# A head's values are split inside the head that uses them, and the attention weights' tiles are taken later

## The chip, the cores and the metric

The kernel runs on one core of one Trainium2 chip. The metric is the device time of one execution in microseconds (us), as the median of several runs. Short names in what follows: PE is TensorE (matmuls), PEld its weight loads, DVE is VectorE, ACT is ScalarE, POOL is GpSimd, SP is SyncE, whose queue issues most of the loads.

## The reference

One step of a two-layer trunk over a prompt of 512 frames and eight samples of 16 frames each. Layer 0 is a gated linear recurrence. Its output is projected once to keys and values, and layer 1 is stick-breaking attention over 16 heads of 128 columns. The change touches only layer 1's attention. Cut to that:

```python
def sb_block(q, q_pos, k, v):
    z = einsum('bqhd,bshd->bhqs', q, k) * HEAD_DIM ** -0.5
    mask = arange(S)[None, :] < q_pos[:, None]
    log_keep  = where(mask, log_sigmoid(-z), 0.0)
    log_after = cumsum(log_keep, axis=3, reverse=True) - log_keep
    attn = where(mask, exp(log_sigmoid(z) + log_after), 0.0)
    return einsum('bhqs,bshd->bqhd', attn, v)

def stick_breaking_mixer(hn, k_all, v_all, w_in, w_out):
    q, zg = split(hn @ w_in, 2)
    o = stick_breaking(heads(q), k_all, v_all)
    return (o * silu(zg)) @ w_out
```

The prompt attends to itself (512 keys). Each sample attends to 512 cached keys and its own 16.

## The kernel before

Every float32 product that has to be exact is made of three matmuls. An operand x is split into a high part xh, which ACT writes as a rounded copy, and a low part xl = x - xh, which DVE writes by a subtraction; `mm3` then adds sh·mh, sh·ml and sl·mh. A split is therefore always one ACT copy and, behind it, one DVE subtraction.

`heads` runs the 16 heads one after the other. The work of a head is cut into steps with one-letter names, and two strings, `ORDER` for heads 0 to 14 and `LAST` for head 15, write out in which order they are traced. The letters:

- P (`prompt_scores`): the scores of the prompt in three matmul groups z3, z2, z1, and for each the chain `sticks`: on ACT Abs, Exp, Ln; on DVE an add, a scan and a subtraction; on ACT the closing Exp (L1664, kept in `self.weighed`); on POOL a mask. The results are the tiles e3, e2, e1.
- q: the next piece of the generator `query(h + 1)`, the product of the next head's query and gate. Its matmuls carry the name psh. A piece gets its weights from splits (L1376 to L1380) that the function `fill` issues ahead. Partial sums leave PSUM by copies on ACT (L1542, `keep`) or sums on DVE (L1547, `evac`), and the PSUM bank is written again by the next partial product.
- c and C (`sample_close`), X (`new_scores`), S0 and S1 (`sample_scores`, again with the chain of `sticks`), V (`prompt_turn`: e3, e2, e1 are transposed on PE and split into the tiles ath and atl, L1748 and L1749), T (`sample_turn`), O (`prompt_out`: the product of ath, atl with the values vh, vl), M (`sample_out`).
- L, K: the next head's keys are loaded and split. U: the next head's values are loaded (`values_load`, L1682, tile vr). W: the next head's values are split (`values_split`, L1326 and L1328, tiles vh and vl). N: the first cached keys of the next head are loaded.

The tile vr of the loaded values has the tag ath and that tag has one buffer. So the values' load can only start when O has read the attention weights of the same head out of it, and the attention weights of the next head can only be written when the values have been split out of it.

A framework keeps the order: each engine works its queue first in, first out; the queues are filled by priority, which follows the order of tracing (raised within `high_priority`), with its own estimate of when things are ready. `issue_after(x)` puts the instructions of a block behind x on x's engine. `self.scaled` is the last copy of the next query on ACT (L1460), `self.weighed` the latest closing Exp.

In the kernel before, W stands near the end of a head, between N and the last q, and its copy is to come behind `self.scaled`. On ACT's queue it has landed behind the first Abs of the next head's P.

Of the kernel before, what the change touches and what calls it, by code (L numbers as in the profile page):

```python
# [13 lines left out]
F32R = mybir.dt.float32r  # L14
# [6 lines left out]
P = 128  # L21
# [4 lines left out]
T = 640  # L26
# [20 lines left out]
X12, X22, X11, S1, S2, S3, S4 = range(7)  # L47
# [4 lines left out]
class Trunk:  # L52
# [12 lines left out]
    def ring(self, tag, bufs, name):  # L65
        return self.pp.tile([P, 512], F32, tag=tag, name=name, bufs=bufs)
# [701 lines left out]
    S0 = 3 + TP  # L768
# [932 lines left out]
    def attention(self, h, ap, qkv, zs):  # L1701

        nc, I, O = self.nc, self.I, self.O
        V, A, mm, tr = nc.vector, nc.scalar, nc.tensor.matmul, nc.tensor.transpose
# [2 lines left out]
        one = self.bank  # L1707
        zt = lambda n: self.ring("quad", 4, n)
        pd = "p (t d) -> p t d"
        qh, ql, qs, kh, kl, knT, vh, vl = qkv  # L1710

        def score(out, i, first):
            q = slice(P * i, P * i + P)
# [1 line left out]
            mm(out, qh[:, q], kh[:, :n], start=first, stop=False, **kw)  # L1715
            mm(out, qh[:, q], kl[:, :n], start=False, stop=False, **kw)
            mm(out, ql[:, q], kh[:, :n], start=False, stop=True, **kw)

        ath = ap.tile([P, 2 * T], F32R, tag="ath", name="ath", bufs=1)
        atl = ap.tile([P, 2 * T], F32R, tag="atl", name="atl", bufs=1)  # L1720

        def turned(x, i):

            if i == 0:
                return x[:, 0:P]
            return x[:, P:].rearrange("p (m s) -> p m s", s=FIRST)[:, : min(i + 1, 3), P * (i - 1) : P * i]

        def block(x, i):

            return x[:, 896:1024] if i == 3 else x[:, TP * i : FIRST * i + TP]  # L1730

        def spread(e, *rows, ring=one):

            ps = ring("pa")
            n = sum(i + 1 for i in rows)
            for j in range(n):
                tr(ps[:, P * j : P * j + P], e[:, P * j : P * j + P], self.ident)
            parts, c = [], 0
            for i in rows:
                m = min(i + 1, 3)  # L1740
                src = ps[:, c : c + P * m]
                parts.append((src.rearrange(pd, d=P) if i else src, turned(ath, i), turned(atl, i)))
                if i == 3:
                    parts.append((ps[:, 384:], block(ath, 3), block(atl, 3)))
                c += P * (i + 1)
            with self.tc.high_priority(200):
                for sv, hv, lv in parts:
                    self.turned = A.activation(hv, sv, AF.Copy).ins  # L1748
                    V.tensor_tensor(lv, sv, hv.bitcast(F32), ALU.subtract)  # L1749
# [15 lines left out]
        def new_values():  # L1765
            t = ap.tile([TS, NB, P], F32, tag="vn", name="vn", bufs=1)
            dma(t, O["v"][TP:, P * h : P * h + P].rearrange("(b t) d -> t b d", t=TS))
            return t
# [84 lines left out]
            A.activation(zn, ps[:, : 2 * TS], AF.Copy)  # L1853

        def prompt_turn():
            spread(st["e3"], 3)
            spread(st["e2"], 2, 0)
            spread(st["e1"], 1, ring=zt)

        def prompt_out():  # L1860
            po = zt("po")
            for i in range(3, -1, -1):
                th, tl = block(ath, i), block(atl, i)
                self.mm3(po[:, P * i :], vh[:, i, :], vl[:, i, :], th, tl, i == 3, i == 0, **kw)
            V.tensor_tensor(o[:, :TP], po, zs[:, :TP], ALU.mult)
# [3 lines left out]
        if h == NHEAD - 1:  # L1869
            o = self.outs.tile([P, 2, 3 * HALF], F32R, tag="ks1", name="o", bufs=1)[:, 0, :T].bitcast(F32)  # L1870
        st = {"vn": new_values()}
        steps = {"P": prompt_scores, "V": prompt_turn, "X": new_scores, "O": prompt_out, "T": sample_turn, "M": sample_out, "C": sample_close}
        for g in range(2):
            steps[f"S{g}"] = lambda g=g: sample_scores(g)
# [2 lines left out]

    STAY = (NHEAD - 2,)
    WHOLE = tuple(range(14))
    LAST = "P c X S0 q q q S1 V q q q q Z T O M q C q"  # L1880
    ORDER = "P q q c X S0 q q q S1 V q q L q T O U K M N W q"

    def heads(self, count=NHEAD):
        with self.pool("att") as ap:
            self.attention_consts(ap)
            self.qraw, self.qready = [None] * 4, {"wh": [], "wl": []}
            for i in (0, 1, 3, 2):
                self.query_load(0, i)
            self.qplan = {"wh": self.product_plan(), "wl": self.plain_plan()}
            out = self.attention_begin()  # L1890
            keys = self.keys_load(0, ap)
            self.ck = self.cached_keys(0, 0, ap)
            self.first_query(ap)
            values = self.values_load(0, ap)
            k, v = self.keys_split(ap, keys), self.values_split(ap, values)
            before = {}
            for h in range(count):
                qh, ql, qs, zs = self.q
                steps = self.attention(h, ap, (qh, ql, qs, *k, *v), zs)
                more = h + 1 < count  # L1900
                qn = self.query(h + 1, ap) if more else out
                if not more:
                    self.behind = self.turned
                for step in (self.ORDER if more else self.LAST).split():
                    if step == "q":
                        next(qn, 0)
                    elif step == "Z":
                        for j in range(2):
                            self.silu(ap, zs, j)
                    elif step in steps:  # L1910
                        steps[step]()
                    elif step == "c":
                        before.get(step.upper(), lambda: None)()
                    elif more and step == "L":
                        keys = self.keys_load(h + 1, ap)
                    elif more and step == "U":
                        values = self.values_load(h + 1, ap)
                    elif more and step == "N":
                        self.ck = self.cached_keys(h + 1, 0, ap)
                    elif more and step == "K":  # L1920
                        with self.tc.issue_after(self.weighed):
                            k = self.keys_split(ap, keys)
                    elif more:
                        with self.tc.issue_after(self.scaled):
                            v = self.values_split(ap, values)
                before = steps
        return out

# [111 lines left out]
def lay_out(r):  # L2040

    heads = lambda v, b: v.reshape(b, -1, NHEAD, P)
    y, k, v = r["y"], r["kT"].T, r["v"]
    state = r["state"].transpose(2, 1, 0).reshape(36, DR)
    out = [y[:TP].reshape(1, TP, D), y[TP:].reshape(NB, TS, D), heads(k[:TP], 1), heads(v[:TP], 1), heads(k[TP:], NB),
           heads(v[TP:], NB), state[0:1].reshape(1, 1, DR), state[1:9].reshape(1, NB, DR),
           state[9:12].reshape(1, 1, 3, DR), state[12:].reshape(1, NB, 3, DR)]
    return tuple(np.ascontiguousarray(v) for v in out)
# [14 lines left out]
```

## Time and profile before

| | |
|---|---|
| median of 3 runs | 2855.23 us (2852.07 to 2855.8) |
| profiled execution | 2849.34 us, its span 2847.6 us |
| granted TensorE clock, mean | 0.997 |
| PE, DVE, ACT busy over the span | 97%, 71%, 58% |
| attention heads 1 to 14 | from 2048.5 to 2600.5 us of the span, 37.6 to 41.5 us each |
| in these 552.0 us | PE busy 536.1 us, DVE 416.4 us, ACT 359.7 us |

The page's busy shares are means over stages with different limits; the heads are the stage that the change touches. In a view by windows each row is a stretch of time with the busy time of each engine in it. In a timeline each row is an instruction: start, duration, engine, line, operation, tiles, and in brackets how long its engine sat idle before it and what ended the wait. A row of the waits names who waited for whom, the sum in us, the number of times and the longest. ACT and DVE instructions are shown with overlapping ends: the next one starts before the shown end of the one before.

### The profile page before, as it was taken

Reading aid. Unit: us, or ns where it says so; the run is one execution under the profiler, and the core shown is the slowest. Engines: PE = TensorE matmul, PEld = TensorE weight load, DVE = VectorE, ACT = ScalarE, POOL = GpSimd, SP = SyncE. Lnnn points to the kernel's source line nnn. Section 1 sums busy time; section 2 is a strip of 40 time slices with the busy share of each in tenths; the row PEclk is TensorE's granted clock in tenths of the full one; section 3 lists DMA queues with packets and bytes.
Section 4 is the critical chain, followed back from the end, with each engine's and each line's share of the span. In section 5 each row is a group of like instructions: output and inputs, shape, how many; then the busy total and the mean of one; then the engine's idle time right before and its main releaser. Section 6 shows DMA issues by size and latency. Waiting matters only on the chain.

```text
span 2847.6 us, 47819 instructions
## 1 busy us (share of the span) xinstructions
PE 2775.1 (97%) x18340; PEld 2457.2 (86%) x18340; DVE 2031.0 (71%) x3312; ACT 1656.7 (58%) x2846; POOL 414.1 (15%) x702
## 2 busy tenths in 40 slices
PE   6999999999999999999999999999999999999998
PEld 4799999999999987777787899967898888987887
DVE  7677776777677765766866866667877777778335
ACT  5467555666566555765756555553666666667223
POOL 0012222222122211111120000122100000001000
PEclk9999999999999999999999999999999999999999
DMA  8966676667666666585686333585465665658536
GB/s 314 343 145 149 166 164 159 150 161 164 161 154 157 157 209 215 192 261 171 222 297 218 102 108 115 174 271 200 137 197 174 203 182 171 194 176 282 165 110 229
DMA packets 244166, 535.31 MB, mean 188 GB/s; under 512 B 22536, under 2 KB 106632, under 8 KB 242784
## 3 DMA queue, kind: packets, MB, share of 16 engines
q1 hardware_dynamic: 198320, 372.99, 41.5%
q0 software_dynamic: 45616, 159.26, 22.9%
q8 instruction: 144, 2.36, 0.3%
q14 instruction: 86, 0.70, 0.1%
HBM read 495.39 MB, written 36.78 MB: 187 GB/s over the span
## 4 chain that ended last, share of the span: by engine, by line
PE 78%; DVE 5%; DMA 4%; ACT 3%; issue 2%; POOL 0%; SPq 0%; DVEq 0%; POOLq 0%; ACTq 0%
PE acc L112 6%; PE acc L114 6%; PE acc L113 6%; PE pa L112 4%; PE pa L114 4%; PE pa L113 4%; PE psh L112 4%; PE psh L114 3%; PE psh L113 3%; PE pc L114 3%; PE pc L112 3%; PE pc L113 3%; DMA vr<-out_v_dram 3%; PE acck L112 3%; PE acck L113 2%; PE acck L114 2%
## 5 line engine op out<-in xcount | busy, mean ns | idle before, releaser
L112 PE MATMUL acc<-wh,yh 128*128 128x512 f32 x940 | 370.2, 394 | 0.0
L113 PE MATMUL acc<-wl,yh 128*128 128x512 f32 x940 | 366.5, 390 | 1.5 <-DVE wl L98 1.5
L114 PE MATMUL acc<-wh,yl 128*128 128x512 f32 x940 | 365.5, 390 | 1.3 <-DVE yl L969 1.3
L98 DVE TENSOR_TENSOR wl<-wr,wh 128x1024 fp32r<-128x1024 f32 x151 | 186.0, 1237 | 208.5 <-ACT wh L97 208.3
L97 ACT ACTIVATE wh<-wr 128x1024 fp32r<-128x1024 f32 x151 | 159.7, 1058 | 259.5 <-PE acc L114 213.1
L112 PEld LDWEIGHTS acc<-wh,yh 128*128 128x128 f32 x940 | 176.4, 188 | 53.6 <-issue 16.7
L113 PEld LDWEIGHTS acc<-wl,yh 128*128 128x128 f32 x940 | 176.5, 188 | 38.9 <-DVE wl L98 3.5
L114 PEld LDWEIGHTS acc<-wh,yl 128*128 128x128 f32 x940 | 176.4, 188 | 38.7 <-DVE yl L969 1.7
L202 DVE TENSOR_TENSOR wa<-wa 128x1024 bf16<-128x1024 f32 (+1 forms) x160 | 191.3, 1247 | 8.9 <-ACT wa L201 8.5
L114 PE MATMUL pa<-xs,wl 128*128 128x320 f32 x630 | 194.8, 309 | 0.5 <-DVE wl L98 0.5
L113 PE MATMUL pa<-xs,wh 128*128 128x320 f32 x630 | 194.7, 309 | 0.0
L112 PE MATMUL pa<-xs,wh 128*128 128x320 f32 x630 | 194.7, 309 | 0.0
L97 ACT ACTIVATE wh<-sum 128x896 fp32r<-128x896 f32 x102 | 96.8, 949 | 143.7 <-PE pa L113 46.8
L201 ACT ACTIVATE wa<-wa 128x1024 bf16<-128x1024 f32 x160 | 159.3, 1046 | 23.0 <-DVE wa L202 11.4
L112 PE MATMUL psh<-nh,wl 128*128 128x320 f32 x480 | 149.8, 312 | 1.9 <-DVE z L1547 1.9
L553 POOL DMA_DIRECT2D sum<-w_in_a_dram x90 | 79.1, 882 | 497.8 <-DVE wl L98 211.2
L114 PE MATMUL psh<-nh,wl 128*128 128x320 f32 x480 | 148.3, 309 | 0.0
L113 PE MATMUL psh<-nl,wl 128*128 128x320 f32 x480 | 148.3, 309 | 0.0
L97 ACT ACTIVATE wh<-rv 128x256 fp32r<-128x256 f32 (+1 forms) x108 | 51.8, 479 | 146.1 <-PE pa L113 95.8
L114 PE MATMUL pc<-xs,wl 128*128 128x320 f32 x420 | 129.8, 309 | 0.7 <-DVE wl L98 0.7
L112 PE MATMUL pc<-xs,wh 128*128 128x320 f32 x420 | 130.0, 310 | 0.0
L113 PE MATMUL pc<-xs,wh 128*128 128x320 f32 x420 | 129.8, 309 | 0.0
(490 smaller groups left out, 8538.3 us busy)
## 6 DMA issues: line engine op xcount, KB each, us to landing
wa<-w_ada_dram POOLq DMA_DIRECT2D x120, 512.0 KB, 5.0
wr<-w_out_a_dram SPq DMA_DIRECT2D x96, 512.0 KB, 4.3
sum<-w_in_a_dram POOLq DMA_DIRECT2D x90, 448.0 KB, 5.6
wa<-w_ada_dram SPq DMA_DIRECT2D x72, 512.0 KB, 6.8
wr<-w_in_b_dram SPq DMA_DIRECT2D x64, 512.0 KB, 4.4
ck<-cache_k_dram SPq DMA_DIRECT2D x64, 512.0 KB, 5.8
wr<-w_out_b_dram SPq DMA_DIRECT2D x55, 512.0 KB, 3.9
raw<-w_in_a_dram SPq DMA_DIRECT2D x60, 448.0 KB, 4.4
```

The source lines that it names most:

```text
L97: self.split_at = nc.scalar.activation(hi[:, :n], raw, AF.Copy).ins
L98: nc.vector.tensor_tensor(lo[:, :n], raw, hi[:, :n].bitcast(F32), ALU.subtract)
L112: mm(out, sh, mh, start=start, stop=False, **kw)
L113: mm(out, sh, ml, start=False, stop=False, **kw)
L114: return mm(out, sl, mh, start=False, stop=stop, **kw)
L201: nc.scalar.activation(parts[i], raw, AF.Copy)
L202: nc.vector.tensor_tensor(parts[2] if i else raw, raw, parts[i], ALU.subtract)
L553: self.nc.gpsimd.dma_start(self.big[tag], self.quarter(w, i), accum_op=ALU.add)
```

## The change

The step W moves from the end of head h - 1, where it split the values of head h, to head h itself, right behind P in `ORDER` and in `LAST`. It is now traced also for head 0, whose split stood ahead of the loop, and its copy comes behind `self.weighed`, which at that place is the closing Exp of e1, the last of the prompt's three chains. The load U stays where it was. The tiles ath and atl are taken at the start of V and no longer at the head's start, since vr now holds the buffer until W.

```diff
-        qh, ql, qs, kh, kl, knT, vh, vl = qkv
+        qh, ql, qs, kh, kl, knT = qkv
...
-        ath = ap.tile([P, 2 * T], F32R, tag="ath", name="ath", bufs=1)
-        atl = ap.tile([P, 2 * T], F32R, tag="atl", name="atl", bufs=1)
...
+            ath, atl = st["at"]
             parts, c = [], 0
...
         def prompt_turn():
+            st["at"] = [ap.tile([P, 2 * T], F32R, tag=tag, name=tag, bufs=1) for tag in ("ath", "atl")]
             spread(st["e3"], 3)
...
             po = zt("po")
+            (ath, atl), (vh, vl) = st["at"], self.v
...
-    LAST = "P c X S0 q q q S1 V q q q q Z T O M q C q"
-    ORDER = "P q q c X S0 q q q S1 V q q L q T O U K M N W q"
+    LAST = "P W c X S0 q q q S1 V q q q q Z T O M q C q"
+    ORDER = "P W q q c X S0 q q q S1 V q q L q T O U K M N q"
...
-            k, v = self.keys_split(ap, keys), self.values_split(ap, values)
+            k = self.keys_split(ap, keys)
...
-                steps = self.attention(h, ap, (qh, ql, qs, *k, *v), zs)
+                steps = self.attention(h, ap, (qh, ql, qs, *k), zs)
...
-                    elif more:
-                        with self.tc.issue_after(self.scaled):
-                            v = self.values_split(ap, values)
+                    elif step == "W":
+                        with self.tc.issue_after(self.weighed):
+                            self.v = self.values_split(ap, values)
```

## The prediction

> **What bounds the kernel now.** I read the page first, then the heads by windows, then PE's waits in them, then one head's timeline engine by engine.
>
> ```profile
> span 2847.6 us, 47819 instructions
> PE 2775.1 (97%) x18340; PEld 2457.2 (86%) x18340; DVE 2031.0 (71%) x3312; ACT 1656.7 (58%) x2846; POOL 414.1 (15%) x702
> ...
> PE 78%; DVE 5%; DMA 4%; ACT 3%; issue 2%; POOL 0%; SPq 0%; DVEq 0%; POOLq 0%; ACTq 0%
> ```
>
> PE is busy nearly all the time, so a change of order can only win back PE's idle time. The chain that ended last is 78% PE, but 4% of it is DMA. The heads by windows, cut at the issue of each head's load of values:
>
> ```profile
> core 0: us, PE busy (x) PEld busy (x) DVE busy (x) ACT busy (x) POOL busy (x), PEclk, DMA share, GB/s
> 2127.23:2166.18 38.95, 38.23 (x346) 34.65 (x338) 29.81 (x56) 25.57 (x60) 2.88 (x8) 1.00 0.63 188
> 2403.49:2444.96 41.47, 39.61 (x346) 35.93 (x338) 29.89 (x56) 25.78 (x60) 2.88 (x8) 0.96 0.59 177
> 2562.89:2600.50 37.61, 37.07 (x298) 33.43 (x290) 28.37 (x50) 25.21 (x54) 2.99 (x8) 1.00 0.85 268
> sum 552.00, PE 536.09 PEld 485.12 DVE 416.39 ACT 359.73 POOL 40.94; mean PE 38.29 PEld 34.65 DVE 29.74 ACT 25.69 POOL 2.92
> ```
>
> In heads 1 to 14 PE is idle for 552.00 - 536.09 = 15.9 us. Who ends that idle time (the waits of that stretch; the first two rows are PE's, the third is ACT's):
>
> ```profile
> PE psh L112 <- ACT qr L1542: 14.7, 13, 1.9
> PE z L1715 <- ACT kh L1326: 0.8, 1, 0.8
> ACT vh L1326 <- DMA vr<-out_v_dram: 22.9, 14, 2.5
> ```
>
> One wait is 14.7 of the 15.9 us: a psh matmul waits, once in each of 13 heads, for a copy on ACT (L1542) that empties its PSUM bank. I call that copy p5, by its name in `query`. Why p5 is late is seen in one head, that of 2127.23 (rows of SP, ACT, PE and DVE):
>
> ```profile
> 2127.23 0.43 SPq L1682 DMA_DIRECT2D vr<-out_v_dram  x1
> ...
> 2130.43 0.58 ACT L1652 ACTIVATE e<-z 128x512 f32<-128x512 f32 x1
> 2132.34 0.63 ACT L1326 ACTIVATE vh<-vr 128x512 fp32r<-128x512 f32 x1 [1.32 <-DMA vr<-out_v_dram]
> 2132.87 0.62 ACT L1653 ACTIVATE e<-e 128x512 f32<-128x512 f32 x1
> ...
> 2137.29 0.63 ACT L1664 ACTIVATE e<-e 128x512 f32<-128x512 f32 x1 [0.33 <-DVE e L1663]
> 2137.83 0.42 ACT L1542 ACTIVATE qr<-psh 128x320 f32<-128x320 f32 x1
> ...
> 2143.09 0.42 ACT L1664 ACTIVATE e<-e 128x256 f32<-128x256 f32 x1 [0.88 <-DVE e L1663]
> 2143.42 0.61 ACT L1379 ACTIVATE wh<-wr 128x512 fp32r<-128x512 f32 x1
> ...
> 2145.56 0.64 ACT L1654 ACTIVATE e<-e 128x528 f32<-128x528 f32 x1
> ...
> 2138.30 0.41 PE L112 MATMUL psh<-ks,wh 128*128 128x320 f32 x1 [0.71 <-ACT qr L1542]
> ...
> 2145.22 0.41 PE L112 MATMUL psh<-nh,wl 128*128 128x320 f32 x1
> ...
> 2133.00 0.69 DVE L1328 TENSOR_TENSOR vl<-vr,vh 128x512 fp32r<-128x512 f32 x1 [1.95 <-ACT vh L1326]
> 2142.64 0.42 DVE L1663 TENSOR_TENSOR e<-z,e 128x256 f32<-128x256 f32 x1
> 2144.07 0.69 DVE L1380 TENSOR_TENSOR wh<-wr,wh 128x512 fp32r<-128x512 f32 x1 [0.81 <-ACT wh L1379]
> 2144.67 0.48 DVE L1547 TENSOR_TENSOR z<-psh,qr 128x320 f32<-128x320 f32 x1
> ```
>
> Read from the top: the load of the values is issued at 2127.23, when the head before has let go of the buffer. ACT does the first Abs of the chain of e3 (2130.43) and then stands for 1.32 us before vh, since the load has not landed; behind vh wait the Exp, the Ln and so the whole chain of e3, and behind its closing Exp (2137.29) waits p5 (2137.83). PE could have gone on at 2138.30 - 0.71 = 2137.59.
>
> **The change, part by part.** *The wait for the load leaves the head of ACT's queue.* Ahead of p5, ACT loses the stall and the copy vh, which holds the queue for 2132.87 - 2132.34 = 0.53 us. In this head p5 comes 1.32 + 0.53 = 1.85 us earlier. PE's wait follows the stall closely; the longest and the shortest pair:
>
> ```profile
> 2409.74 0.63 ACT L1326 ACTIVATE vh<-vr 128x512 fp32r<-128x512 f32 x1 [2.48 <-DMA vr<-out_v_dram]
> 2415.70 0.41 PE L112 MATMUL psh<-ks,wh 128*128 128x320 f32 x1 [1.86 <-ACT qr L1542]
> ...
> 2567.59 0.63 ACT L1326 ACTIVATE vh<-vr 128x512 fp32r<-128x512 f32 x1 [0.91 <-DMA vr<-out_v_dram]
> 2573.55 0.41 PE L112 MATMUL psh<-ks,wh 128*128 128x320 f32 x1 [0.30 <-ACT qr L1542]
> ```
>
> 1.86 = 2.48 - 0.62, 0.30 = 0.91 - 0.61, and above 0.71 = 1.32 - 0.61. So the wait is the stall less 0.61 us, and with stall and copy gone p5 is 0.61 + 0.53 = 1.14 us early in every head. All 13 waits go: -14.7 us. The 0.8 us of head 1 (it waits for keys, not values) stays.
>
> *A slow stretch behind the longest wait.* In the head of 2403.49 PE's busy time is 39.61 against 38.23 us in that of 2127.23, and its clock 0.96:
>
> ```profile
> 2412.00:2416.00 4.00, 2.14 (x15) 1.88 (x14) 3.90 (x6) 3.67 (x9) 0.43 (x1) 1.00 0.69 168
> 2416.00:2420.00 4.00, 4.00 (x38) 3.27 (x36) 3.96 (x7) 1.11 (x3) 0.30 (x1) 0.57 0.01 2
> ```
>
> The clock falls to 0.57 for 4 us right behind that head's wait of 1.86 us, and in the other two heads shown in the windows with shorter waits it is 1.00. I take the wait to be its cause: 39.61 - 38.23 = 1.38 us go with it. Bounds: 0 (it has another cause) and 1.38. [...]
>
> *The split at its new place.* It is the same copy and the same subtraction, 0.53 us of ACT's queue and some 0.60 of DVE's (2144.67 - 2144.07, a subtraction of the same size), behind the closing Exp of e1 (2143.09). No DMA is issued by it and SP's queue keeps its order. What stands behind it on ACT is the copy of the weights wh (2143.42), behind that on DVE their subtraction (2144.07), and behind that on DVE the sum at 2144.67, which ends at 2145.15 and empties the bank that PE's group of 2145.22 writes. PE reaches that group 2145.22 - 2138.30 = 6.92 us behind p5's matmul, so this sum is already now just in time: it is what is late next. Placed afresh, with the stall gone: the chain's end moves 1.85 us up, the subtraction of e1 to 2140.79 and the Exp to 2141.24; vh 0.33 us later at 2141.57, wh at 2142.10, ready at 2142.71; vl on DVE from 2142.25 to 2142.85, in the time in which DVE waits for wh anyway (it idled 0.81 there before); the subtraction of wh at 2142.85, the sum from 2143.45 to 2143.93. PE needs it at 2137.59 + 6.92 = 2144.51. It has 0.58 us to spare, so I take the new place at nothing. Bounds: -0.1 us a head (PE's start at 2145.22 comes 0.07 us behind the sum, a hair that may go) and the rivals below. If that cover is gone, what is beyond 0.58 us is paid 13 times.
>
> *The values and the tiles.* vr lands by 2132.34 at the latest in this head and is now read at 2141.57, so the load has 9 us to spare. The first users:
>
> ```profile
> 2152.38 0.50 ACT L1748 ACTIVATE ath<-pa 128x384 fp32r<-128x384 f32 x1 [0.56 <-PE pa L1737]
> ...
> 2162.65 0.30 PE L112 MATMUL po<-ath,vh 128*128 128x128 f32 x1
> ```
>
> ath is first written at 2152.38, 9.5 us behind the placed end of vl, and vh is first read at 2162.65. At V, ACT waited for PE's transposes (0.56 us), so the rest of the head runs at PE's pace and takes no harm. Cost of both: 0, with cover of 9 us.
>
> *Heads 0 and 15.* They have the same edit but not the same wait:
>
> ```profile
> 2018.39 0.61 ACT L1326 ACTIVATE vh<-vr 128x512 fp32r<-128x512 f32 x1
> ...
> PE psh L112 <- DVE z L1547: 1.9, 1, 1.9
> PE psh L112 <- ACT wh L1379: 0.7, 1, 0.7
> ...
> 2605.93 0.63 ACT L1326 ACTIVATE vh<-vr 128x512 fp32r<-128x512 f32 x1 [1.98 <-DMA vr<-out_v_dram]
> ...
> PE acc L113 <- DVE wl L98: 0.8, 1, 0.8
> ```
>
> In head 0 ACT does not wait for the load, and PE's wait of 1.9 us is for the gate's sum on DVE, which stands ahead of the split; the 0.7 us for a weights' copy behind it may go or grow by the 0.53 us that the copy vh moves. In head 15 ACT waits 1.98 us, but PE's matmuls there are mostly the output product's, and its longest wait is 0.8 us, for a split of other weights. I take 0 for each, bounds -0.7 and +0.6 for head 0, -0.8 and +0.6 for head 15.
>
> *Sum.* -14.7 - 1.4 = -16.1 us. The profiled execution of 2849.34 would take 2833.2 us. The median of the runs, 2855.23, lies 5.9 us above it and shows no reason; I take the same 16.1 us off: 2839.1 us, 0.56% less. If part of those 5.9 us are further long waits or dips of this kind, they go too: down to 2833.
>
> **The rivals.** *The sum on DVE becomes the new lock (2847 us).* The queue order is the framework's; one more pair of a copy and a subtraction ahead of the sum at 2144.67, 0.53 + 0.60 us later than placed, eats the 0.58 us and leaves PE waiting some 0.55 to 0.6 us in each of 13 heads: 7 to 8 us back, 2839.1 + 7.8 = 2847. For it: the sum ends 0.07 us ahead of its use today. Against: DVE idles 0.81 us right there.
>
> *It is slower (2866 us).* The split's copy is held only behind the Exp of e1; should it be queued on ACT behind the sample's first activations too, while its subtraction keeps its place on DVE ahead of wh, all of DVE stands behind it. The Ln of those activations started at 2145.56; 1.85 us up and 0.55 us of queue later vh would start at 2144.26 and end at 2144.87, vl end its turn at 2145.5, wh's subtraction at 2146.1 and the sum at 2146.6, against 2144.5: PE waits 2.1 us a head, 13 x 2.1 = 27 us in place of 16.1, so 2855.2 + 11 = 2866. It turns to a loss when the sum ends later than 2144.51 + 16.1 / 13 = 2145.75. Against it: the split is traced ahead of the sample's scores and so has the higher priority.
>
> *It doesn't do what it says (2854 us).* The copy p5 stays late since other ACT work takes the freed place ahead of it: it needs over 1.14 us more, three copies of 0.53 us, to leave PE waiting at all, and about 2.3 us to leave today's mean of 14.7 / 13 = 1.13 us. For it: p5 already stands behind work that came ready later than it. Against: its copy has a raised priority.
>
> **How the numbers follow.** The forecast of 2839 us has 0.74, with its own range of 2833 to 2845; the new lock on DVE 0.12; no effect 0.06; slower 0.08. About 0.2% (5.7 us) is what a measurement can tell here, so faster means below 2849.5. Faster: 0.74 + 0.10 of the 0.12 = 0.84; within 0.2%: 0.02 + 0.06 = 0.08; slower 0.08. The range from 2832 to 2851 holds the first two cases, the bounds of the dip and of heads 0 and 15.
>
> **What would show it.** ACT's wait for vr is gone from the waits (22.9 us to under 1), PE's wait of psh for L1542 too, and the heads take 38.2 to 38.4 us each with a clock of 1.00. vh stands behind the third closing Exp and ahead of a wh copy. Wrong would be: a wait of PE for DVE's L1547 in every head (the first rival), an idle DVE ahead of vl for over 1.5 us (the second), or psh still waiting for L1542 (the third).

## The result, and the profile after

The changed kernel takes 2832.39 us (median of 6 runs, 2828.62 to 2835.09) against 2852.36 us (6 runs, 2851.81 to 2855.8) of the kernel before: 20.0 us less, a ratio of 0.9926 with a 95% interval of 0.9914 to 0.9939 (the ratios here are taken over all runs and differ a little from those of the medians). Forecast were 16.1 us less, 2839.1 us, with a range of 2833 to 2845 us for this case. In a second timing on one chip the same two kernels stood at 2829.26 and 2849.46 us, ratio 0.993 (0.9917 to 0.9944), 20.2 us apart. The mechanism came as forecast, its size did not.

One agreement is luck. The two profiled executions, 2849.34 and 2833.32 us, are 16.0 us apart, just what the forecast said of them. But in the heads 21.15 us went; the stages ahead of them, which the change leaves alone, took 2052.34 - 2048.14 = 4.20 us longer in the second profile, and the tail behind them 0.95 us longer.

The heads in windows, cut at the issue of each head's load of values. First the whole stretch from the load of head 1's values to that of head 15's, before and after, then two heads after (columns as in the prediction):

```profile
2048.14:2600.50 552.36, 536.45 (x4729) 485.48 (x4727) 416.75 (x766) 360.09 (x826) 40.94 (x112) 1.00 0.64 191
```
```profile
2052.34:2583.55 531.21, 530.34 (x4731) 484.43 (x4729) 414.79 (x767) 360.53 (x828) 41.81 (x112) 1.00 0.67 199
2130.42:2168.28 37.86, 37.86 (x346) 34.63 (x338) 29.71 (x56) 25.57 (x60) 2.95 (x8) 1.00 0.67 193
2395.53:2433.41 37.88, 37.88 (x346) 34.64 (x338) 29.71 (x56) 25.56 (x60) 2.94 (x8) 1.00 0.66 194
```

The stretch is 21.15 us shorter; a head (2 to 13) takes 37.87 us where it took 38.95 to 41.47. PE is busy for all of a head. Look at the second number too: PE's busy time fell from 536.45 to 530.34 us with the same matmuls in it (the counts differ by two of over 4700 records). The forecast had taken it to be fixed, apart from the slow stretch. What PE still waits for in this stretch of the changed kernel, and what ACT waits for of DMAs:

```profile
PE z L1715 <- ACT kh L1326: 0.7, 1, 0.7
PE pos L1794 <- ACT e L1780: 0.2, 1, 0.2
...
ACT yh L968 <- DMA yl<-odl: 1.3, 1, 1.3
ACT kh L1326 <- DMA kr<-out_kT_dram: 1.2, 1, 1.2
```

PE's 13 waits for the copy p5 (14.7 us) and ACT's for vr (22.9 us) are gone. One head of the changed kernel, rows of ACT, DVE and PE:

```profile
2133.62 0.58 ACT L1652 ACTIVATE e<-z 128x512 f32<-128x512 f32 x1
...
2138.70 0.42 ACT L1542 ACTIVATE qr<-psh 128x320 f32<-128x320 f32 x1
...
2139.53 0.62 ACT L1664 ACTIVATE e<-e 128x512 f32<-128x512 f32 x1
...
2144.40 0.42 ACT L1664 ACTIVATE e<-e 128x256 f32<-128x256 f32 x1 [0.88 <-DVE e L1663]
2144.72 0.62 ACT L1326 ACTIVATE vh<-vr 128x512 fp32r<-128x512 f32 x1
2145.24 0.62 ACT L1379 ACTIVATE wh<-wr 128x512 fp32r<-128x512 f32 x1
...
2145.37 0.69 DVE L1328 TENSOR_TENSOR vl<-vr,vh 128x512 fp32r<-128x512 f32 x1 [1.01 <-ACT vh L1326]
2145.98 0.69 DVE L1380 TENSOR_TENSOR wh<-wr,wh 128x512 fp32r<-128x512 f32 x1
2146.58 0.29 DVE L1811 TENSOR_TENSOR z<-pot,z 128x128 f32<-128x128 f32 x1
2146.78 0.48 DVE L1547 TENSOR_TENSOR z<-psh,qr 128x320 f32<-128x320 f32 x1
...
2147.43 0.31 PE L112 MATMUL psh<-nh,wl 128*128 128x320 f32 x1
```

The split stands where it was meant to, behind the closing Exp of e1 and ahead of the copy wh. Two things are not as in the forecast. p5 (2138.70) now stands ahead of the closing Exp of e3 (2139.53), since the framework filled the queue otherwise. It needn't have: right behind that Exp, which holds the queue for 0.54 us in the kernel before, it would end at 2139.53 + 0.54 + 0.42 = 2140.49, still 0.12 us ahead of PE's group of 2140.61 (shown below). That is worked out from the rows and was not run. And the sum that was late next ends at 2146.78 + 0.48 = 2147.26, 0.17 us ahead of the group that needs it (2147.43), and not 0.58 us.

### The profile page after: what moved, and what is told of

The parts are those of the page before. It is cut to its first block, busy times and chain, and to the rows that moved or that the text cites. A ratio compares the mean times of both kernels' runs of the same rounds, so it can differ in the third digit from the quotient of the medians.

```text
span 2831.6 us, 47815 instructions
## 1 busy us (share of the span) xinstructions
PE 2773.7 (98%) x18340; PEld 2459.4 (87%) x18340; DVE 2029.1 (72%) x3312; ACT 1657.0 (59%) x2846; POOL 419.6 (15%) x702
## 4 chain that ended last, share of the span: by engine, by line
PE 83%; DVE 3%; issue 2%; ACT 2%; DMA 2%; POOL 1%; SPq 0%; DVEq 0%; POOLq 0%; ACTq 0%
PE acc L112 7%; PE acc L114 6%; PE acc L113 6%; PE pa L112 4%; PE psh L112 4%; PE psh L114 4%; PE psh L113 4%; PE pa L114 4%; PE pa L113 4%; PE pc L114 3%; PE pc L112 3%; PE pc L113 3%; PE acck L112 3%; PE acck L113 3%; PE acck L114 3%
## 5 line engine op out<-in xcount | busy, mean ns | idle before, releaser
L201 ACT ACTIVATE wa<-wa 128x1024 bf16<-128x1024 f32 x160 | 159.8, 1047 | 25.6 <-DVE wa L202 12.2
L98 DVE TENSOR_TENSOR wl<-sum,wh 128x896 fp32r<-128x896 f32 x102 | 110.9, 1087 | 27.3 <-ACT wh L97 27.0
L112 PE MATMUL pc<-xs,wh 128*128 128x320 f32 x420 | 130.0, 310 | 0.0
```

The source lines that it names most:

```text
L98: nc.vector.tensor_tensor(lo[:, :n], raw, hi[:, :n].bitcast(F32), ALU.subtract)
L112: mm(out, sh, mh, start=start, stop=False, **kw)
L201: nc.scalar.activation(parts[i], raw, AF.Copy)
```

## The experiments

**The wait or the place?** The kernel before, with a buffer of its own for vr and the load traced beside the keys' load; the split stays ahead of the prompt's chains.

```diff
-        tile = ap.tile([P, 2 * T], F32R, tag="ath", name="vr", bufs=1).bitcast(F32)
-        raw = tile[:, :TP].rearrange("p (t d) -> p t d", d=P)
+        tile = ap.tile([P, TP], F32, tag="vr", name="vr", bufs=1)
+        raw = tile.rearrange("p (t d) -> p t d", d=P)
...
-            an = st["an"] = ap.tile([TS, 2 * P], F32, tag="an", name="an", bufs=1)
+            an = st["an"] = ap.tile([P, 2 * P], F32, tag="ob", name="an", bufs=1)[0:TS, :]
...
-    ORDER = "P q q c X S0 q q q S1 V q q L q T O U K M N W q"
+    ORDER = "P q q c X S0 q q q S1 V q q L U q T O K M N W q"
```

> The kernel before, with a buffer of its own for the loaded values and the load traced beside the next head's keys (step U behind L); the split stays at the old place, ahead of the prompt's chains. (To make room, the two small sample tiles an and ob share one buffer.) Theory: the stall of ACT for the load is the whole cause, the place of the split is not. Then ACT waits for vr under 2 us in all (22.9 before), PE's wait of psh for the copy L1542 goes in heads 2 to 14 since p5 is late only by the stall less 0.61 us, these heads take 37.9 to 38.1 us, and the time falls by 18 to 21 us, as with the whole change. Rival: the copy of 0.53 us ahead of the prompt's chain is part of the cause; then some 0.4 us or more a head stay and the time falls by 10 to 15 us only. Rival 2: an earlier load collides with the cached values on the DMA queues, and the fall is under 8 us.

It takes 2827.31 us against 2849.99 us of the kernel before on the same chip: 22.7 us less, a little more than expected, ratio 0.9925 (0.9909 to 0.9941), that of the whole change within the intervals. What ACT and DVE still wait for at the split (from the view of the tile vr), p5 and the closing Exp of e3 in one head, and PE over twelve heads:

```profile
  DMA vr<-out_v_dram: 0.5, 1
...
2130.86 0.42 ACT L1542 ACTIVATE qr<-psh 128x320 f32<-128x320 f32 x1
...
2131.70 0.62 ACT L1664 ACTIVATE e<-e 128x512 f32<-128x512 f32 x1
...
2087.75:2542.28 454.53, 454.53 (x4058) 415.67 (x4057) 356.59 (x661) 308.00 (x708) 35.49 (x96) 1.00 0.66 194
```

ACT waited for vr once, 0.5 us, and PE has no idle time at all: 454.53 / 12 = 37.88 us a head. So the stall for the load was the cause; the place of the split, ahead of or behind the chains, is worth nothing that these times show. The rival that the 0.53 us of the copy are part of it falls. This kernel doesn't take the tiles ath and atl later either, so that part of the change isn't needed for the gain. One thing is not separated: p5 moved ahead of the closing Exp here too. Placed behind it as above, p5 would end some 0.15 us ahead of its use in eleven of the twelve heads, and 0.2 us behind it in one. What p5's new place is worth with the stall left in was not run by itself; in the kernel with three copies, below, p5 stands there too, ACT still waits 22.7 us for vr, and with its two more copies a head that kernel is no faster than the one before.

**What is late next.** The changed kernel with the split done twice.

```diff
                         with self.tc.issue_after(self.weighed):
+                            self.values_split(ap, values)
                             self.v = self.values_split(ap, values)
```

> The changed kernel with the split of the values done twice at its new place (the first result is written over). Theory: the sum on DVE (L1547, z) that empties PE's bank ends only 0.17 us ahead of its use in the changed kernel, so one more copy of 0.53 us and one more subtraction of 0.60 us on the way to it are paid: PE waits 0.4 to 0.6 us a head for L1547 in 13 heads, 5 to 8 us more than the changed kernel, heads of 38.3 to 38.5 us. Rival: the split is hidden at its new place with room to spare, 0 to 1 us more, heads of 37.9 us.

2835.26 us, ratio 0.9952 (0.994 to 0.9964) to the kernel before; the changed kernel's 0.9926 and 0.993 lie below that interval, though their own intervals reach up to it or just into it. PE's waits in the heads, one head, and in it the second vl, the sum and PE:

```profile
PE psh L112 <- DVE z L1547: 5.0, 14, 0.6
...
2130.28:2168.74 38.46, 38.15 (x346) 34.63 (x338) 30.31 (x57) 26.11 (x61) 2.96 (x8) 1.00 0.66 190
...
2146.64 0.69 DVE L1328 TENSOR_TENSOR vl<-vr,vh 128x512 fp32r<-128x512 f32 x1
2147.24 0.49 DVE L1547 TENSOR_TENSOR z<-psh,qr 128x320 f32<-128x320 f32 x1
...
2147.78 0.41 PE L112 MATMUL psh<-nh,wl 128*128 128x320 f32 x1 [0.31 <-DVE z L1547]
```

The sum on DVE is the next lock, as expected: 0.6 us more ahead of it and PE waits in every head. Mark the size: the head is 38.46 - 37.87 = 0.59 us longer, but the wait shown is 0.31. The missing 0.28 us are the point on which the forecast failed, below. From the load of head 1's values to that of head 15's this profile takes 539.03 us, 7.8 more than the changed kernel's.

**More room for the sum.** The changed kernel with the split behind the first sample group's chain.

```diff
-    LAST = "P W c X S0 q q q S1 V q q q q Z T O M q C q"
-    ORDER = "P W q q c X S0 q q q S1 V q q L q T O U K M N q"
+    LAST = "P c X S0 W q q q S1 V q q q q Z T O M q C q"
+    ORDER = "P q q c X S0 W q q q S1 V q q L q T O U K M N q"
```

> The changed kernel with the split behind the first sample group's chain (step W behind S0, its copy behind that chain's closing Exp), where DVE idles 1.3 us in each head. Theory: PE has no idle time left in heads 2 to 14, so these stay at 37.8 to 37.9 us and the time is that of the changed kernel within 2 us, though the sum L1547 now ends earlier than 0.17 us ahead of its use. Rival: the sum L1547 is already a lock in some heads; then 0.1 to 0.3 us a head come back, 1.5 to 4 us less. Rival 2: the subtraction comes too late for the attention weights at step V and PE waits there: 3 us or more longer.

2832.91 us, ratio 0.9939 (0.9927 to 0.9951), an interval that overlaps with both of the changed kernel's; that kernel itself was not timed on this chip. Against the doubled split on the same chip it is only 2.35 us less, although its heads 1 to 14 are 8.3 us shorter in the profile: its tail had a wait of 2.2 us for a mask on POOL (next experiment), the other's had none. The same head, the sum and the group that needs it:

```profile
2130.27:2168.15 37.88, 37.88 (x346) 34.65 (x338) 29.71 (x56) 25.55 (x60) 2.95 (x8) 1.00 0.64 193
...
2145.83 0.48 DVE L1547 TENSOR_TENSOR z<-psh,qr 128x320 f32<-128x320 f32 x1
...
2147.29 0.31 PE L112 MATMUL psh<-nh,wl 128*128 128x320 f32 x1
```

The sum now ends at 2146.31, 0.98 us early and not 0.17, and the head takes the same 37.88 us, with no idle time of PE. By these two signs the sum cost nothing more in the changed kernel.

**Head 15.** In the changed kernel's profile the tail, from the load of head 15's values to the end, was 2831.6 - 2583.55 = 248.05 us against 2847.6 - 2600.50 = 247.10 before, with a new wait in it (rows of POOL, the head's two sample masks, of PE, and two windows):

```profile
2606.03 1.02 POOL L1668 TENSOR_TENSOR e<-e,mask 128x16 f32<-128x16 f32 x1 [6.97 <-PE acc L114]
2612.87 5.80 POOL L1668 TENSOR_TENSOR e<-e,mask 128x16 f32<-128x16 f32 x1 [5.82 <-ACT e L1664]
...
2618.73 0.28 PE L1783 MATMUL pan<-ident,e 128*16 128x128 f32 x1 [1.68 <-POOL e L1668]
...
2615.00:2619.00 4.00, 2.33 (x16) 1.82 (x15) 3.60 (x4) 2.92 (x4) 3.68 (x1) 1.00 0.73 240
2619.00:2623.00 4.00, 4.00 (x25) 2.92 (x23) 0.41 (x1) 0.00 (x0) 0.00 (x0) 0.70 0.81 286
```

Not only the changed kernel has it: the kernel with the split behind the sample's chain waited 2.2 us there, and the kernel before with five copies, below, 1.4 us. The experiment puts these masks of head 15 on DVE.

```diff
-            nc.gpsimd.tensor_tensor(v, v, m, ALU.mult)
+            (masker or nc.gpsimd).tensor_tensor(v, v, m, ALU.mult)
...
-            st[f"es{g}"] = self.sticks(ap, [(zc, 0), (zn, PAST)], PAST + TS, [(0, PAST + TS, 1)])
+            st[f"es{g}"] = self.sticks(ap, [(zc, 0), (zn, PAST)], PAST + TS, [(0, PAST + TS, 1)], V if h == NHEAD - 1 else None)
```

> The changed kernel, with the two masks of the sample's chains in head 15 on DVE and no longer on POOL. Theory: in head 15 of the changed kernel the POOL mask of 128x16 took 5.8 us while DVE ran without a pause (0.2 us in the other heads), PE waited 1.7 us for it and the clock fell to 0.70 and 0.90 behind that wait; on DVE the mask takes 0.2 us, so 1.7 to 3.5 us less than the changed kernel in executions in which that wait came up. Rival: the mask's shown span is no more than a rough record and PE's wait is for something else that ends then, 0 us.

2826.83 us, ratio 0.9918 (0.9905 to 0.993), tail 245.89 us. The changed kernel was not timed on that chip, so both were timed once more on one:

> The changed kernel itself, timed beside e5's kernel on one chip. Theory: 2829 to 2835 us, with PE's wait of 1.5 to 2.3 us for the POOL mask in head 15 in the profile, and heads 2 to 13 of 37.87 us.

> The changed kernel with the sample's masks of head 15 on DVE, again, now on the same chip as the changed kernel. Theory (the mask on POOL starves while DVE works without a pause, PE waits for it and its clock halves for a few us behind the wait): 2 to 4 us less than the changed kernel. Rival (the first difference was the chip's): within 1 us.

The changed kernel took 2829.26 us, with 0.8 us of wait for the mask, where 1.5 to 2.3 had been expected, and a tail of 245.74 us; with the masks on DVE it took 2827.32 us, ratio 0.9921 (0.9906 to 0.9936), and the wait for POOL is gone (tail 245.17 us). 1.9 us are just short of the 2 to 4 expected and too few for the intervals to tell apart. That the wait is there and goes with the mask is shown; that this version beats the changed kernel is not.

**Does the clock fall behind an idle stretch?** The kernel before, with the copy vh made three times (the edit shown), and five times.

```diff
-        return self.split(ap, "v", [P, 4, P], raw, 1)
+        hi = ap.tile([P, 4, P], F32R, tag="vh", name="vh", bufs=1)
+        lo = ap.tile([P, 4, P], F32R, tag="vl", name="vl", bufs=1)
+        for _ in range(3):
+            self.nc.scalar.activation(hi, raw, AF.Copy)
+        self.nc.vector.tensor_tensor(lo, raw, hi.bitcast(F32), ALU.subtract)
+        return hi, lo
```

> The kernel before with the copy vh made three times in place of once (the same result is written over), so 1.06 us more on ACT ahead of the prompt's chains in each head: PE's wait for the copy L1542 grows to 1.4 to 2.9 us in heads 2 to 14. Theory (the halved clock follows an idle stretch of 1 to 2 us of PE, in some executions and not in others): at least 4 of these 13 waits are followed by a stretch of some 3.4 us at half clock, and the heads in which that is so take 1.4 to 2 us longer than the others with the same wait. [...]

> The kernel before with the copy vh made five times, 2.1 us more on ACT ahead of the prompt's chains: PE's wait for L1542 grows to 2.4 to 4.0 us in heads 2 to 14. Theory: most of the 13 waits are followed by a stretch at half clock. [...]

One execution of each: 2854.86 and 2856.86 us. The first told nothing on the question: p5 was put ahead of the closing Exp here as well, so PE waited at most 1.1 us for it (5.3 us in 9 heads) and some 1 us for the sum on DVE (12.2 us in 13), and the clock stayed at 1.00 in all these heads. In the second, waits for p5 reached 2.2 us. Two of its heads, the wait and the clock behind it:

```profile
2176.84 0.41 PE L112 MATMUL psh<-ks,wh 128*128 128x320 f32 x1 [2.02 <-ACT qr L1542]
...
2178.00:2180.00 2.00, 2.00 (x9) 1.68 (x7) 1.87 (x5) 1.97 (x6) 0.00 (x0) 0.50 0.00 0
...
2298.32 0.41 PE L112 MATMUL psh<-ks,wh 128*128 128x320 f32 x1 [2.20 <-ACT qr L1542]
...
2299.00:2301.00 2.00, 2.00 (x32) 1.61 (x34) 2.00 (x4) 1.97 (x6) 0.00 (x0) 1.00 0.00 0
```

Of six waits from 1.28 to 2.20 us, those of 2.02 and 1.95 us were followed by half clock, that of 2.20 us was not. My "most of the 13" was wrong. A cleaner count is in head 0, where every kernel here waits the same 1.9 us for a sum on DVE: in six of the ten profiles (the changed kernel, its repetition, and four experiments) the clock fell to 0.50 behind it for about 3.4 us, in four, the kernel before among them, it did not. The pair of the kernel after and the kernel before:

```profile
2021.92 0.41 PE L112 MATMUL psh<-nh,wl 128*128 128x320 f32 x1 [1.94 <-DVE z L1547]
...
2024.00:2026.00 2.00, 2.00 (x8) 1.81 (x7) 0.69 (x1) 1.32 (x3) 0.00 (x0) 0.50 0.32 124
```
```profile
2017.96 0.41 PE L112 MATMUL psh<-nh,wl 128*128 128x320 f32 x1 [1.94 <-DVE z L1547]
...
2020.00:2022.00 2.00, 2.00 (x13) 1.91 (x14) 1.20 (x2) 1.87 (x4) 0.00 (x0) 1.00 0.29 112
```

Which waits are hit can be read off the traces. In each of the ten profiles the changes of the granted clock stand whole multiples of 3.4133 us apart (in the kernel before it fell to 0.50 at 101.94 and at 2416.17 us, 678 times that length later), so I cut the time into windows of that length, in the heads ahead of a dip as well. Such windows of the kernel after (head 0), of the kernel before (head 0), and around the wait of 2.20 us above:

```profile
2019.86:2023.28 3.42, 1.48 (x13) 1.36 (x10) 3.42 (x9) 1.43 (x4) 0.00 (x0) 1.00 0.86 225
2023.28:2026.69 3.41, 3.41 (x14) 3.23 (x13) 1.28 (x2) 2.01 (x4) 0.00 (x0) 0.50 0.41 159
```
```profile
2016.81:2020.22 3.41, 2.26 (x13) 2.03 (x14) 3.41 (x8) 2.15 (x6) 0.00 (x0) 1.00 0.80 283
2020.22:2023.63 3.41, 3.41 (x24) 3.32 (x24) 1.58 (x3) 3.30 (x7) 0.00 (x0) 1.00 0.43 124
```
```profile
2293.77:2297.18 3.41, 2.35 (x17) 2.08 (x15) 2.51 (x3) 3.11 (x7) 0.00 (x0) 1.00 1.04 258
2297.18:2300.59 3.41, 2.27 (x24) 2.10 (x27) 2.47 (x5) 3.28 (x8) 0.43 (x1) 1.00 0.02 6
```

In the first, all 1.94 us of idle time lie in one window and the next runs at half clock. In the other two an edge cuts the wait, no window holds more than 1.15 us of it, and the clock stays. So it is in all ten heads 0: in the six that are hit the wait lies in one window, in the four others it is cut. From 150 to 2790 us of the ten profiles PE stood idle for 1.8 us or more of a window 13 times, and 12 of the next windows ran at half clock. Of the windows with less, one was followed by half clock (1.54 us); it and the one of the 13 that was not (1.95 us) are both at the POOL mask of head 15.

The tiles taken later, without the move of the split, were not run.

## Why the prediction was right and where it was wrong

**The stall and its removal: right.** All 13 waits went, by the cause named, as the kernel with a buffer of its own shows. That p5 also changed its place in the queue was not forecast; by the rows it wasn't needed.

**The term of 14.7 us: the step that failed.** It was too small: the 13 waits and what hung on them cost some 19.5 us. The forecast summed the idle times that the waits print. Around one of them in the kernel before, at 2138.30, stand these rows, and the last is the one behind the group of 2145.22:

```profile
2137.13 0.31 PE L113 MATMUL psh<-nl,wl 128*128 128x320 f32 x1
2137.28 0.31 PE L114 MATMUL psh<-nh,wl 128*128 128x320 f32 x1
...
2138.55 0.30 PE L113 MATMUL psh<-ks,wh 128*128 128x320 f32 x1
...
2145.47 0.31 PE L113 MATMUL psh<-nl,wl 128*128 128x320 f32 x1
```

and in the changed kernel at the same place:

```profile
2140.47 0.31 PE L114 MATMUL psh<-nh,wl 128*128 128x320 f32 x1
2140.61 0.31 PE L112 MATMUL psh<-ks,wh 128*128 128x320 f32 x1
```

These matmuls of 320 columns start 0.15 us apart and are drawn 0.31 us long. Idle time is counted from the drawn end, so 0.16 us of each wait are covered by it: from start to start PE lost 2138.30 - 2137.28 - 0.15 = 0.87 us, not 0.71. The matmul behind the wait (drawn 0.41 us) and the one behind it are 0.25 us apart, 0.10 more. And at the group of 2145.22 another 0.10 were lost in the same way, where the sum came just in time; the forecast had seen that one and left it out as a bound. Together 0.37 us a head: 13 x 0.37 = 4.8. With it the sum is 14.7 + 4.8 + 1.4 = 20.9 us, against the 21.15 us measured in that stretch. The 0.28 us that the doubled split cost beyond its shown wait are the same thing once more. The 536 us of PE's busy time were therefore no floor: 6.1 us of them went, some 4.8 of waiting and 1.4 of the slow stretch, and the heads took 37.87 us and not the 38.2 to 38.4 forecast.

**The dip of the clock, 1.4 us: right for the profiled execution.** The wait of 1.86 us lay in one window of the clock and was followed by half clock (0.50 from 2416.17 to 2419.59); the next longest of the kernel before, 1.78 and 1.64 us, were not. Heads 2 to 14 of the changed kernel and its variants, with no idle stretch above 0.6 us, show no dip. How often a run of the kernel before is hit was not measured, so what this term is worth in the median stays open. In head 0 an idle stretch of 1.9 us was followed by half clock in six of the ten profiles and not in the four others.

**The split's new place at nothing: right, but closer than worked out.** 0.17 us were left of the 0.58. The small sum of 2146.58, which now comes between, takes 2146.78 - 2146.58 = 0.20 us of the difference. The rest is the failed step again: the forecast let PE go on at 2137.59, by the drawn end, where 2137.28 + 0.15 = 2137.43 was due, and gave it 6.92 us from there to the group, which include 0.10 of the restart; in the changed kernel they are 2147.43 - 2140.61 = 6.82. So PE needs the sum some 0.26 us sooner. The doubled split shows the rival's price: 0.59 us a head.

**Heads 0 and 15 at nothing.** Head 0 kept its wait; from its load of values to the next it took 33.2 us before and 33.5 in both profiles of the changed kernel, in which a dip stands behind the wait; that is within the bounds. Head 15 got a new wait, for POOL, that no row of before had shown: 0.8 and 1.7 us in two profiles, the second beyond the 0.6 us that the forecast allowed, with a dip behind it.

**The median.** Profiles of these kernels reach the first load of values at 2011.4 to 2020.2 us of the span (leaving out the one that issues it elsewhere), in stages that the change leaves alone, and eleven runs of the kernel before on one chip lay between 2843.29 and 2853.08 us. Such a spread is enough for the 5.9 us by which the first profile lay under its median (3.0 us under that of the six runs); more to win in the heads need not stand behind it.

## What to carry to other kernels

Count a wait of TensorE from start to start against the usual distance of its matmuls, not by the idle time that is shown: here each wait cost 0.27 us more than shown, and a sum that ended 0.07 us ahead of its use cost 0.10 us with no wait shown at all. Here a wait could cost more than its length by the clock (1.38 us of busy time went with one of 1.86 us): what counted was whether 1.8 us or more of PE's idle time fell into one window of 3.41 us, and 12 of 13 such windows were followed by half clock. A copy that waited for its load held up what stood behind it in ACT's queue: in the kernel before ACT waited 22.9 us for vr and PE 14.7 us for p5 behind it; loading earlier (ratio 0.9925) and using later (0.9926 and 0.993) were worth the same within the intervals. When an engine's queue order changes, look also at the last stage, where the neighbours differ.

## What the runs showed of the hardware

A mask of 128x16 on POOL took 0.2 to 0.3 us in the other heads. In head 15, where DVE worked without a pause (back to back from 2603.75 to 2618.61), the changed kernel's two masks took 1.02 and 5.80 us; in the second profile of that kernel the later one took 4.66 us. Each of these ended less than 0.1 us behind the end of a DVE instruction, but not of the first one: eight of DVE's were under way or begun during the 5.80 us. No pause of DVE stands at that end in the second profile: the mask ended at 2613.04, in the midst of three subtractions that DVE ran back to back until 2614.12:

```profile
2608.38 4.66 POOL L1668 TENSOR_TENSOR e<-e,mask 128x16 f32<-128x16 f32 x1 [5.08 <-ACT e L1664]
...
2610.62 3.50 DVE L98 TENSOR_TENSOR wl<-wr,wh 128x1024 fp32r<-128x1024 f32 x3
```

So such a mask took 4.66 and 5.80 us beside several DVE instructions in a row. What holds it, why it ends behind one of them and not behind another, and why the kernel before's masks there took only 0.75 and 0.24 us, isn't shown.
